# The ConvFFN of layer 0 by seven block products instead of eight, on one Trainium2 core

## The chip, the core and the metric

The kernel runs on one core of one Trainium2 chip. The metric is device time in microseconds for one execution, from the inputs in DRAM to the output in DRAM. The kernel before took 1979.17 us, the median of three runs (1978.67 to 1980.45). Engines are named as in the profile: PE (matmul), DVE, ACT, POOL (GpSimd), and SP, whose queue issues every DMA of this kernel.

## The reference

The network has two layers over 512 latent tokens and 256 context tokens of width 1024. Layer 0 mixes tokens by attention and a short convolution, layer 1 by a state-space scan; after each mixer comes a ConvFFN. The change is in the ConvFFN of layer 0, which works on all 768 tokens:

```python
def _convffn(x, w_up, conv_w, w_down):      # d = 1024, D_FF = 2816
    u = _dwconv(x @ w_up, conv_w)           # 768 x 5632, three taps along the tokens
    a, g = jnp.split(u, 2, axis=-1)         # two halves of 2816
    return (jax.nn.silu(a) * g) @ w_down    # 768 x 1024
```

Its input is normed and modulated (a scale and a shift per feature, one pair for latent and one for context tokens); its output is normed, gated and added to the stream. The modulation vectors come from products of the condition vectors with `mod_w`; those of layer 1 and the last of layer 0 are computed by the kernel while other work runs.

## The kernel before, in words

**Precision.** Every large product is made of three: each operand is held as a high part (fp32r, rounded by ACT) and the rest (low = operand − high, by DVE), and `mm3` (L133) adds high·high, high·low and low·high in PSUM. `split` (L141) is one ACT copy and one DVE subtraction; both write the arena `arena_r`, while loaded data and intermediates stand in `arena_f`. A 128 x 1024 weight block of 512 KB comes by one DMA into a ring of four slots, `self.raw`, and is split from there.

**Order.** The code is written in program order, and a scheduler sets the order on each engine. Each engine then runs its list in order: an instruction that waits holds up all behind it, and so does a DMA issue on SP.

**Side work.** `mod_tile` (L253) loads a 512 KB block of transposed `mod_w` and makes one multiply-and-sum on DVE (L259) per condition. A generator hands these out: `set_fill` names the chunks, `pump` takes the next tile, and `drain` takes all that are left. `mod_rows` (L302) does the same by matmuls with 32 columns for three chunks of layer 0, during the input projections.

**Input projections of layer 0 (93 to 230 us).** Twelve feature blocks of 128 columns, `proj(6)` to `proj(17)`, over all 768 tokens; each takes one 512 KB block `hyb_w` and 24 matmuls of 512 and 24 of 256 columns. `pump` between them takes two `mod_rows` steps for each group of three blocks.

**ConvFFN of layer 0, `ffn(0)` (456 to 1009 us).** The feature blocks come in 22 pairs (p and 22 + p). For each block `gemm_fm` takes the 8 blocks of the contraction and the 768 tokens as 512 + 256 columns: 48 matmuls in PSUM. From PSUM, ACT applies the middle tap and DVE the two others (`taps`, one instruction of 511 and one of 255 columns per tap). ACT makes the silu and DVE the product, then split. Groups of 2 to 4 pairs are multiplied at once with their rows of `ffn_down` (6 token tiles x 2 halves of 512 columns), and DVE adds the result to `macc`. All features stay in SBUF. `pump(2)` after each block takes two mod tiles. At the start, the transposed input comes in two calls of `to_hT`: four token tiles at the end of `mixer0`, two in `rest_hT` inside `ffn`. `ffn(1)` runs the same code on 512 tokens.

Of the kernel before, what the change touches and what calls it, by code (L numbers as in the profile page):

```python
# [93 lines left out]
class Kern:  # L94
# [27 lines left out]
    def dma(self, out, in_):  # L122
        return self.nc.sync.dma_start(out=out, in_=in_).ins
# [6 lines left out]
    def mm(self, out, a, b, start, stop):  # L130
        self.nc.tensor.matmul(out, a, b, start=start, stop=stop)  # L131

    def mm3(self, out, a, b, start, stop):  # L133
        self.mm(out, a[0], b[0], start, False)
        self.mm(out, a[0], b[1], False, False)
        self.mm(out, a[1], b[0], False, stop)
# [60 lines left out]
    def build(self):  # L197
        tc = self.tc
        with ExitStack() as ctx:
# [13 lines left out]
            self.yd = dram.tile([2 * D, NL], F32, name="y_dram")  # L213
            b = Bump(self.F, 0, self.NF)
# [25 lines left out]
            self.sinks()  # L240
            self.mixer0()
            if self.stop == "mix0":
                return
            self.ffn(0)
# [5 lines left out]
            self.ffn(1)  # L250


    def mod_tile(self, l, j, f, conds, cols):  # L253

        r = self.raw()
# [70 lines left out]

    def set_fill(self, chunks):
        def gen():
            for ch in chunks:
                yield from self.mod_chunk(*ch)  # L330
        self.drain()
        self.fill = gen()
# [62 lines left out]
    def mixer0(self):  # L395
# [148 lines left out]
        self.fill = self.mod_rows((4, 3, 2), cc)  # L544
# [56 lines left out]
        self.banks((0, 2, 4), (6, 7))  # L601
        rq = rows(0, 384)
# [24 lines left out]
        for j in range(4):  # L627
            ps = proj(6 + 3 * j)
            gc = tmp()
            self.act(gc, ps, AF.Copy)  # L630
            self.pump(j > 0)
            ps = proj(7 + 3 * j)
            u = tmp()
            self.tt(u, ps, gc, ALU.mult)
            y = conv32[j]
            wc = self.scw[:, 3 * j:3 * j + 3]
            self.act(y, u, scale=wc[:, 1:2])
            self.taps(y, u, wc, SEGS)
            ps = proj(8 + 3 * j)
            self.tt(y, ps, y, ALU.mult)  # L640
            self.pump(j < 3)
# [138 lines left out]
        tm2 = b.ring(512, 3)  # L780
# [32 lines left out]
        hT2 = HT(R, 8, 0, 32 * KB)  # L813
# [13 lines left out]
        for t in range(6):  # L827
            pss[t] = wo_tile(t, w1)
            if t < 4:
                fin(t)  # L830
        self.to_hT(m0[:4], hT2, 0, 1, 0, tm2)
        for t in (4, 5):
            fin(t)
        self.hT = hT2
        self.rest_hT = lambda: self.to_hT(m0[4:], hT2, NL, 1, 1, tm2, par=1)
        self.upw = [108 * KB, wb, wb + 2048]
        self.set_fill([(0, 5, (0, 1)), (1, 1, (0, 1)), (1, 0, (0, 1)), (1, 4, (0,)), (1, 3, (0,)), (1, 2, (0,)), (1, 5, (0,))])
# [18 lines left out]
    def ffn(self, l):  # L856
        io, R, F, fb = self.io, self.R, self.F, self.fb
        last = l == 1
        ntt = 4 if last else 6
        segs = SEGS[:1] if last else SEGS  # L860
        n = NL if last else NT
        hT = self.hT
        W = Ring(R, self.upw, 2048)
        if last:
            self.sinks(R[:, 120 * KB:])
        else:
            self.sinks(R[:, 104 * KB:108 * KB])
        b = Bump(R, (24 if last else 64) * KB, self.NR)
        gt = [b(2 * n) for _ in range(4)]
        wd = Ring(R, [72 * KB, 80 * KB, 16 * KB] if last else [88 * KB, 96 * KB, 116 * KB], 2048)  # L870
# [5 lines left out]
        th = ring(F, tb + 2048, 512, 2)  # L876
# [7 lines left out]
        parts = ((0, 256), (256, 512)) if last else SEGS  # L884
        ahead = (0, NPAIR, 1, NPAIR + 1) if last else (0, NPAIR, 1)
        slot = ring(self.psa, 0, 512, 5) if last else self.P
# [16 lines left out]
        self.P = Ring(self.psa, [512 * j for j in ((4, 6, 0, 2) if last else (6, 0, 2, 4))], 1024)  # L903

        def up(j):
# [12 lines left out]
            if j not in head:  # L918
                self.pump(2)
# [15 lines left out]
        def down(gi):  # L935
            grp = groups[gi]
            for t in range(ntt):
# [15 lines left out]
                if gi == len(groups) - 1:  # L953
                    finish(t)
                    if not last and t == 3:
                        self.to_hT(macc[:4], hT, 0, 0, 0, th)

        def finish(t):
            c = 0 if t < 4 else 1
# [3 lines left out]
            for h in range(2):  # L963
                s = slice(h * 512, (h + 1) * 512)
                self.tt(m[:, s], m[:, s], self.res[l, 5, c][:, s], ALU.mult, eng=self.nc.gpsimd if h == 0 else None)
                self.stt(x[:, s], m[:, s], r, x[:, s], ALU.mult, ALU.add)
                if last:
                    self.dma(self.out[t * 128:(t + 1) * 128, s], x[:, s])
            self.tap("xf%d" % l, x, slice(t * 128, (t + 1) * 128))
            if not last:  # L970
                if c == 0:
                    self.dma(self.xd[t * 128:(t + 1) * 128, :], x)
                self.norm_tok(m, x)
                if t + 4 < ntt:
                    xs.append(next_x(t + 4))
# [10 lines left out]
        for gi in range(len(groups)):  # L986
# [3 lines left out]
            if not nxt:  # L990
                for c in range(1 if last else 2):
                    self.gate_row(l, 5, c)
# [8 lines left out]
        self.rest_hT = lambda: self.to_hT(macc[4:], hT, NL, 0, 1, th, par=1)  # L1001
# [604 lines left out]
```

## Time and profile before

| | us |
|---|---|
| median of three runs | 1979.17 (1978.67 to 1980.45) |
| the profiled execution | 1985.27 |
| its span | 1983.5 |
| PE busy | 1862.7 (94%) |
| DVE busy | 1295.8 (65%) |
| ACT busy | 869.6 (44%) |
| POOL busy | 457.3 (23%) |
| moved by DMA | 226.13 MB, mean 114 GB/s |

The span runs from the first instruction to the last on the core; the rest of the execution's time lies around it. Busy time is the time in which an engine has at least one instruction running. The share of an engine is an average over stages that have different limits, so the stretches of the kernel are looked at one by one. A row of a group of instructions tells its line, engine, operation, output and inputs, shapes and count, then the total busy time and the mean time of one in ns, then the idle time in front of them and what ended it.

### The profile page before, as it was taken

What the parts mean: (1) busy time and instruction counts of PE and PEld (TensorE: products, weight loads), DVE (VectorE), ACT (ScalarE), POOL (GpSimd) and SP (SyncE); (2) the same over time, 40 slices, a digit from 0 to 9 for tenths busy, and PEclk for the clock granted to TensorE, in tenths of its full rate; (3) what the DMA queues carried; (4) which work ended last, traced back from release to release, by engine and by line L of the source; (5) the groups of instructions that cost most, each with busy time, mean ns of one, the idle gap of its engine ahead of it and who ended that gap; (6) DMA issues with size and microseconds to landing.
All of it is one profiled execution on the core that took longest, in us unless ns stands there. A gap on an engine that the chain in (4) does not pass through costs nothing.

```text
span 1983.5 us, 26291 instructions
## 1 busy us (share of the span) xinstructions
PE 1862.7 (94%) x10184; PEld 1584.8 (80%) x10184; DVE 1295.8 (65%) x1867; ACT 869.6 (44%) x1398; POOL 457.3 (23%) x514
## 2 busy tenths in 40 slices
PE   7999998899999999999989799899998899999998
PEld 3887787778888888888868688888887688888886
DVE  3332488747998667545567888878787476555564
ACT  4421367545422222322356465766664455233332
POOL 1000124111000000000040778777684110000002
PEclk9899999999999999999989989998999999999999
DMA  8155200243555535221222313232234554223322
GB/s 320 54 165 172 81 24 12 62 172 113 185 160 181 159 117 170 85 64 54 91 91 65 109 56 104 87 115 87 95 123 149 188 196 132 75 95 96 96 85 74
DMA packets 72933, 226.13 MB, mean 114 GB/s; under 512 B 9004, under 2 KB 11368, under 8 KB 72808
## 3 DMA queue, kind: packets, MB, share of 16 engines
q1 hardware_dynamic: 72808, 224.45, 34.4%
q8 instruction: 80, 1.31, 0.3%
q14 instruction: 45, 0.37, 0.1%
HBM read 210.63 MB, written 13.79 MB: 113 GB/s over the span
## 4 chain that ended last, share of the span: by engine, by line
issue 47%; PE 24%; POOL 10%; DVE 9%; DMA 5%; ACT 4%; SPq 0%; POOLq 0%; DVEq 0%; ACTq 0%
PE psum L131 23%; POOL arena_f L113 8%; DVE arena_r L113 4%; DVE arena_f L113 2%; ACT arena_f L101 2%; POOL arena_f L1292 2%; DMA arena_f<-a_dram 2%; ACT arena_r L101 1%; PE psum L139 1%; DVE arena_f L107 1%; DVE arena_f L110 1%; DMA y_dram<-arena_f 1%; DVE arena_f L697 1%; ACT junk L101 1%; POOL arena_f L107 1%
## 5 line engine op out<-in xcount | busy, mean ns | idle before, releaser
L131 PE MATMUL psum<-arena_r 128*128 128x512 f32 (+2 forms) x9324 | 1776.9, 350 | 74.4 <-ACT arena_r L101 30.4
L131 PEld LDWEIGHTS psum<-arena_r 128*128 128x128 f32 x9324 | 1504.1, 192 | 323.0 <-ACT arena_r L101 43.3
L101 ACT ACTIVATE arena_r<-arena_f 128x512 fp32r<-128x512 f32 (+5 forms) x545 | 418.5, 794 | 627.1 <-PE psum L131 279.6
L113 DVE TENSOR_TENSOR arena_r<-arena_f,arena_r 128x1024 fp32r<-128x1024 f32 (+4 forms) x497 | 482.4, 988 | 321.2 <-ACT arena_r L101 319.2
L113 POOL TENSOR_TENSOR arena_f<-arena_f 128x256 f32<-128x256 f32 (+5 forms) x330 | 313.3, 972 | 180.9 <-ACT arena_f L101 79.5
L107 POOL TENSOR_SCALAR arena_f<-arena_f 128x1 f32<-128x1 f32 (+2 forms) x88 | 37.7, 429 | 1093.2 <-ACT junk L101 987.6
L113 DVE TENSOR_TENSOR arena_f<-psum,arena_f 128x256 f32<-128x256 f32 (+6 forms) x277 | 173.9, 645 | 124.5 <-PE psum L131 109.6
L110 DVE SCALAR_TENSOR_TENSOR arena_f<-psum,arena_f 128x511 f32<-128x511 f32 (+2 forms) x356 | 217.4, 648 | 51.4 <-ACT arena_f L101 49.1
L101 ACT ACTIVATE arena_f<-psum,arena_f 128x768 f32<-128x768 f32 (+2 forms) x217 | 163.8, 764 | 95.2 <-PE psum L131 41.2
L113 DVE TENSOR_TENSOR arena_f<-arena_f 128x512 f32<-128x512 f32 (+5 forms) x180 | 144.5, 812 | 57.2 <-POOL arena_f L1292 30.1
L101 ACT ACTIVATE arena_f<-arena_f 128x512 f32<-128x512 f32 (+5 forms) x115 | 81.6, 712 | 161.3 <-DVE arena_f L110 93.0
L139 PE MATMUL psum<-arena_f 128*128 128x128 f32 x596 | 94.6, 283 | 33.8 <-DVE arena_f L107 20.9
L101 ACT ACTIVATE arena_f<-psum 128x512 f32<-128x512 f32 (+9 forms) x135 | 72.4, 547 | 97.0 <-PE psum L131 84.8
L139 PEld LDWEIGHTS psum<-arena_f 128*128 128x128 f32 x596 | 71.1, 143 | 51.1 <-DVE arena_f L107 25.8
L259 DVE SCALAR_TENSOR_TENSOR junk<-arena_f 128x1024 bf16<-128x1024 f32 x80 | 97.7, 1221 | 19.4 <-DMA arena_f<-in_mod_t_dram 18.3
L113 POOL TENSOR_TENSOR arena_r<-arena_f,arena_r 128x768 fp32r<-128x768 f32 (+2 forms) x28 | 50.0, 1803 | 247.2 <-ACT arena_r L101 232.4
L107 DVE TENSOR_SCALAR arena_f<-arena_f 128x512 f32<-128x512 f32 (+4 forms) x97 | 55.3, 611 | 28.2 <-POOL arena_f L113 27.5
L101 ACT ACT_TABLE_LOAD x48 | 61.6, 1283 | 22.9 <-DVE arena_f L110 19.5
L101 ACT ACTIVATE junk<-arena_f 128x512 bf16<-128x512 f32 (+1 forms) x76 | 40.4, 533 | 47.2 <-DVE arena_f L113 33.5
L1292 POOL TENSOR_SCALAR_AFFINE_SELECT arena_f<-arena_f 128x512 f32<-128x512 f32 x64 | 59.3, 941 | 0.0
L110 DVE SCALAR_TENSOR_TENSOR arena_f<-arena_f 128x512 f32<-128x512 f32 (+3 forms) x75 | 48.5, 683 | 10.4 <-POOL arena_f L113 5.8
L101 ACT ACTIVATE arena_r<-psum 128x512 fp32r<-128x512 f32 (+2 forms) x72 | 41.2, 591 | 30.0 <-PE psum L139 16.1
(25 smaller groups left out, 249.2 us busy)
## 6 DMA issues: line engine op xcount, KB each, us to landing
arena_f<-in_ffn_up_dram SPq DMA_DIRECT2D x88, 512.0 KB
arena_f<-in_mod_t_dram SPq DMA_DIRECT2D x56, 512.0 KB
arena_f<-in_ffn_down_dram SPq DMA_DIRECT2D x44, 512.0 KB
arena_f<-in_mod_dram SPq DMA_DIRECT2D x40, 512.0 KB
arena_f<-a_dram SPq DMA_DIRECT2D x32, 512.0 KB
arena_f<-in_ssd_w_dram SPq DMA_DIRECT2D x24, 512.0 KB
arena_f<-in_ssd_o_dram SPq DMA_DIRECT2D x24, 512.0 KB
arena_f<-in_ssd_z_dram SPq DMA_DIRECT2D x16, 512.0 KB
```

What stands on the lines that cost most here:

```text
L101: return self.nc.scalar.activation(out=out, in_=in_, func=func, **kw).ins
L107: (eng or self.nc.vector).tensor_scalar(**kw)
L110: self.nc.vector.scalar_tensor_tensor(out=out, in0=in0, scalar=s, in1=in1, op0=op0, op1=op1)
L113: return (eng or self.nc.vector).tensor_tensor(out=out, in0=a, in1=b, op=op).ins
L131: self.nc.tensor.matmul(out, a, b, start=start, stop=stop)
L139: self.nc.tensor.transpose(out, in_, self.ident)
L259: self.nc.vector.scalar_tensor_tensor(out=self.junk2, in0=r, scalar=1.0, in1=self.cb[c], op0=ALU.mult, op1=ALU.mult, accum_out=o)
L697: nc.vector.tensor_reduce(out=nm, in_=ps.rearrange("p (i n) -> p i n", i=2), axis=AX.X, op=ALU.max, negate=True)
L1292: pool.affine_select(out=rd, in_=rd, pattern=[[0, 4], [1 - 2 * d, 128]], compare_op=ALU.is_ge, fill=0.0, base=-d, channel_multiplier=2 * d ...
```

## The change

Both products of the ConvFFN of layer 0 are cut into 2 x 2 blocks, and the four block results are made by seven block products in place of eight (Strassen's scheme in Winograd's form, with the sums of blocks made beforehand). Feature pair p holds the two blocks of the weight's columns, the contraction is halved into 4 + 4 blocks, and the 768 tokens into 384 + 384. So each of the seven products of a pair is 4 contraction blocks of `mm3` with 384 columns: 12 matmuls, 84 per pair.

- **Up.** `hop` holds the input blocks and their four sums, split, for the whole stage; `rest` makes the second half and the sums (DVE, two of the four sums on POOL). For a pair, POOL makes four sums of weight blocks (128 x 512), and ACT and DVE split seven operands. The results leave PSUM by ACT copies and by three DVE operations of 384 columns into a buffer `U`, and the taps read that buffer.
- **Gated features by way of DRAM.** The product `g1` of each pair goes to `gf_dram`; for every second pair POOL makes four sums of 384 columns and they are stored too.
- **Down.** A separate run of 7 x 11 steps after all pairs: a step loads 128 x 512 of the weight (or of its sums) and 128 x 384 of features, splits both, and makes 9 matmuls of 512 columns. `macc` is combined in PSUM and by ACT and DVE after each product. The finishing of the token tiles is written into the seventh product.
- **Sums of the down weight.** `down_forms` makes them during the input projections: 11 steps of two 512 KB loads, four POOL operations of 512 columns and two 512 KB stores to `w_dram`.
- **Side work.** The 24 `mod_rows` loads are taken two steps at a time, between the first projections; two chunks of layer 1 (16 tiles, 32 sums on DVE) follow there, and the last chunk of layer 1 moves to `ffn1`.

```diff
+    def down_forms(self, slots):
+        g = self.nc.gpsimd
+        a, b = slice(0, 512), slice(512, 1024)
+        for i in range(NPAIR // 2):
+            r = [slots(1024) for _ in range(2)]
+            for k in range(2):
+                self.dma(r[k], self.io["ffn_down"][0, (2 * i + k) * 128:(2 * i + k + 1) * 128, :])
+            self.tt(r[1][:, b], r[0][:, b], r[1][:, b], ALU.subtract, eng=g)
+            self.tt(r[0][:, b], r[0][:, a], r[0][:, b], ALU.subtract, eng=g)
...
+            for k in range(2):
+                self.dma(self.wfd[k][i * 128:(i + 1) * 128, :], r[k])
+            yield
...
-        self.fill = self.mod_rows((4, 3, 2), cc)
+        def fills():
+            yield from self.mod_rows((4, 3, 2), cc)
+            yield from self.mod_chunks([(1, 1, (0, 1)), (1, 0, (0, 1))])
+        self.fill = fills()
+        forms = self.down_forms(self.gwr)
...
-            self.pump(j > 0)
+            self.pump(2)
+            next(forms, None)
             ps = proj(7 + 3 * j)
+            self.pump(2)
+            next(forms, None)
...
             ps = proj(8 + 3 * j)
             self.tt(y, ps, y, ALU.mult)
-            self.pump(j < 3)
+            self.pump(2)
+            next(forms, None)
...
+        def rest():
...
+            for f in range(4):
+                b12[f], b22[f] = feat(1, f), feat(1, f + 4)
+                op["3", f] = hl_tile(places[16 + f])
+                self.act(v3(op["3", f][0], 3), b22[f], AF.Copy)
+                self.tt(v3(op["3", f][1], 3), b22[f], v3(op["3", f][0], 3), ALU.subtract)
+                self.tt(b22[f], b12[f], b22[f], ALU.subtract)
+                self.tt(b12[f], mv[0][:, f], b12[f], ALU.subtract, eng=pool)
+                self.tt(mv[0][:, f], b22[f], mv[0][:, f], ALU.subtract)
+                op["6", f] = hl_split(mv[0][:, f], hl_tile(places[f]))
...
-        self.set_fill([(0, 5, (0, 1)), (1, 1, (0, 1)), (1, 0, (0, 1)), (1, 4, (0,)), (1, 3, (0,)), (1, 2, (0,)), (1, 5, (0,))])
+        self.set_fill([(0, 5, (0, 1)), (1, 4, (0,)), (1, 3, (0,)), (1, 2, (0,))])
...
+        def add(i, p):
...
+            self.tt(sums[i, p], x, y, ALU.add, eng=pool)
+        def operand(n):
...
+            w = WS()
+            self.split(src, w[:, a5], w[:, b5])
+            wop[p, i] = w[:, a5], w[:, b5]
+        def product(n):
...
+            for k in range(4):
+                self.mm3(ps, [x[:, k * 128:(k + 1) * 128] for x in w], op[p, k], ...)
...
+        def glu(i):
+            ya, g1 = ys[i, 0], ys[i, 1]
+            self.act(ya, ya, AF.Silu)
+            self.tt(g1, ya, g1, ALU.mult)
...
+            self.tt(x[:, h0], g0[:, h0], g0[:, h1], ALU.add, eng=pool)
+            self.tt(x[:, h1], g0[:, h1], g1[:, h1], ALU.add, eng=pool)
...
+        for n in range(6):
+            operand(n)
+        first = [product(n) for n in range(6)]
...
+        self.rest_hT()
...
+        for n in range(6, len(seq)):
+            for m in range(n, n + 4):
+                operand(m)
...
+            after(p, i, product(n))
+            if p == "2" or n < at["1", 3] and p == "7":
+                self.pump()
...
+        for n, (p, k) in enumerate(steps[:6 * nk]):
+            ahead(n + 5)
...
+            for t in range(3):
+                self.mm3(ps[t], [x[:, t * 128:(t + 1) * 128] for x in g], w, ...)
```

SP, during the input projections: `in_mod_dram` are the `mod_rows` loads, `in_hyb_w_dram` the weight of one projection, `in_ffn_down_dram` and `w_dram` the loads and stores of `down_forms`. Before:

```order
27 L123 DMA arena_f<-in_hyb_w_dram 128x1024
28 L123 DMA arena_f<-in_mod_dram 128x1024 x3
29 L123 DMA arena_f<-in_hyb_w_dram 128x1024
30 L123 DMA arena_f<-in_mod_dram 128x1024 x4
31 L123 DMA arena_f<-in_hyb_w_dram 128x1024 x2
32 L123 DMA arena_f<-in_mod_dram 128x1024 x4
```

and now:

```order
47 L123 DMA arena_f<-in_hyb_w_dram 128x1024
48 L123 DMA w_dram_72<-arena_f 128x1024
49 L123 DMA w_dram_73<-arena_f 128x1024
50 L123 DMA arena_f<-in_mod_dram 128x1024 x3
51 L123 DMA arena_f<-in_ffn_down_dram 128x1024
52 L123 DMA arena_f<-in_mod_dram 128x1024
53 L123 DMA arena_f<-in_ffn_down_dram 128x1024
54 L123 DMA arena_f<-in_mod_dram 128x1024 x4
55 L123 DMA arena_f<-in_hyb_w_dram 128x1024
```

Between two weights of projections there stood three or four loads; now there are eight loads and two stores, and the stores wait for POOL.

DVE, at the start of the ConvFFN: `junk_67` is the output of a mod sum, `128x384` (or `128x3x128`) are splits and sums of the input, `128x512` into `arena_r` splits of weights. Before, from the end of the input's split:

```order
281 L107 TENSOR_SCALAR arena_f<-psum,arena_f 128x256
282 L113 TENSOR_TENSOR arena_r<-arena_f,arena_r 128x256 x3
283 L113 TENSOR_TENSOR arena_r<-arena_f,arena_r 128x1024 x2
284 L110 SCALAR_TENSOR_TENSOR arena_f<-psum,arena_f 128x511
285 L110 SCALAR_TENSOR_TENSOR arena_f<-psum,arena_f 128x255
286 L113 TENSOR_TENSOR arena_r<-arena_f,arena_r 128x1024
```

and now, in the middle of the input's split:

```order
320 L113 TENSOR_TENSOR arena_r<-arena_f,arena_r 128x384 x2
321 L113 TENSOR_TENSOR arena_f<-arena_f 128x3x128
322 L113 TENSOR_TENSOR arena_r<-arena_f,arena_r 128x384
323 L263 SCALAR_TENSOR_TENSOR junk_67,arena_f<-arena_f 128x1024
324 L113 TENSOR_TENSOR arena_r<-arena_f,arena_r 128x384
325 L107 TENSOR_SCALAR arena_f<-psum,arena_f 128x128
326 L113 TENSOR_TENSOR arena_f<-arena_f 128x3x128
327 L113 TENSOR_TENSOR arena_r<-arena_f,arena_r 128x384
328 L113 TENSOR_TENSOR arena_r<-arena_f,arena_r 128x512
329 L263 SCALAR_TENSOR_TENSOR junk_67,arena_f<-arena_f 128x1024
```

The list of this start, from row 285 to row 342 of DVE, has 12 mod sums among 26 splits of 384 columns, 8 sums of 384 columns and 9 splits of weights.

DVE, in the middle of the up product, before:

```order
400 L110 SCALAR_TENSOR_TENSOR arena_f<-psum,arena_f 128x511
401 L110 SCALAR_TENSOR_TENSOR arena_f<-psum,arena_f 128x255
402 L259 SCALAR_TENSOR_TENSOR junk_67,arena_f<-arena_f 128x1024
403 L113 TENSOR_TENSOR arena_f<-arena_f 128x768
404 L113 TENSOR_TENSOR arena_r<-arena_f,arena_r 128x1024
```

and now:

```order
546 L113 TENSOR_TENSOR arena_f<-arena_f 128x768
547 L113 TENSOR_TENSOR arena_r<-arena_f,arena_r 128x512 x3
548 L113 TENSOR_TENSOR arena_f<-psum,arena_f 128x384
549 L113 TENSOR_TENSOR arena_r<-arena_f,arena_r 128x512
550 L110 SCALAR_TENSOR_TENSOR arena_f<-arena_f 128x511
551 L110 SCALAR_TENSOR_TENSOR arena_f<-arena_f 128x255
552 L113 TENSOR_TENSOR arena_r<-arena_f,arena_r 128x512
```

The taps read `arena_f` where they read `psum`, and a pair has seven splits of 512 columns where it had two of 1024; POOL's list, empty there before, has four operations of 512 and on average two of 384 columns per pair.

## Rows read from the trace of the kernel before

**Rows 1.** The page's view of the span in 40 slices (busy tenths).

```profile
PE   7999998899999999999989799899998899999998
DVE  3332488747998667545567888878787476555564
POOL 1000124111000000000040778777684110000002
DMA  8155200243555535221222313232234554223322
```

**Rows 2.** Windows: us, busy us of PE, PEld, DVE, ACT, POOL (x instructions), PEclk, DMA share, GB/s.

```profile
15.00:25.00 10.00, 7.71 (x44) 2.56 (x36) 2.50 (x6) 2.48 (x4) 0.00 (x0) 1.00 1.03 406
100.00:150.00 50.00, 50.00 (x298) 40.69 (x297) 18.62 (x25) 14.79 (x21) 0.00 (x0) 1.00 0.53 167
150.00:200.00 50.00, 50.00 (x308) 39.86 (x307) 13.11 (x18) 9.16 (x13) 0.00 (x0) 1.00 0.52 180
500.00:600.00 100.00, 100.00 (x536) 86.72 (x535) 94.34 (x148) 33.03 (x36) 0.00 (x0) 1.00 0.55 172
700.00:800.00 100.00, 100.00 (x518) 85.94 (x516) 65.67 (x92) 22.12 (x25) 0.00 (x0) 1.00 0.41 132
1100.00:1500.00 400.00, 357.94 (x2258) 321.08 (x2257) 336.73 (x497) 246.95 (x374) 307.37 (x317) 0.94 0.30 97
```

**Rows 3.** Timeline of PE and of DVE around the start of the ConvFFN of layer 0.

```profile
444.64 6.74 PE L131 MATMUL psum<-arena_r 128*128 128x512 f32 x29
456.45 5.76 PE L131 MATMUL psum<-arena_r 128*128 128x512 f32 x24 [0.98 <-DVE arena_r L113]
...
446.75 0.69 DVE L113 TENSOR_TENSOR arena_f<-psum,arena_f 128x512 f32<-128x512 f32 x1 [0.21 <-ACT junk L101]
452.27 0.69 DVE L113 TENSOR_TENSOR arena_f<-psum,arena_f 128x512 f32<-128x512 f32 x1 [0.57 <-ACT junk L101]
```

**Rows 4.** Timeline of PE at the end of it.

```profile
1005.83 3.45 PE L131 MATMUL psum<-arena_r 128*128 128x512 f32 x14
1011.58 0.44 PE L139 MATMUL psum<-arena_f 128*128 128x128 f32 x2 [2.30 <-DVE arena_f L107]
```

**Rows 5.** PE's cost of one matmul: timeline near 1952, groups of 72.9:91.3 and of 100:230.

```profile
1951.70 22.04 PE L131 MATMUL psum<-arena_r 128*128 128x512 f32 x96
...
L131 PE MATMUL psum<-arena_r 128*128 128x256 f32 x120 | 14.8, 284 | 0.4 <-ACT arena_f L101 0.4
...
L131 PE MATMUL psum<-arena_f 128*32 128x512 f32 x96 | 12.2, 601 | 0.0
```

**Rows 6.** Timeline of DVE, two instructions behind one another without a wait.

```profile
524.56 1.22 DVE L113 TENSOR_TENSOR arena_r<-arena_f,arena_r 128x1024 fp32r<-128x1024 f32 x1
525.70 1.22 DVE L259 SCALAR_TENSOR_TENSOR junk<-arena_f 128x1024 bf16<-128x1024 f32 x1
...
539.63 1.14 DVE L110 SCALAR_TENSOR_TENSOR arena_f<-psum,arena_f 128x511 f32<-128x511 f32 x2
540.68 1.22 DVE L259 SCALAR_TENSOR_TENSOR junk<-arena_f 128x1024 bf16<-128x1024 f32 x1
```

**Rows 7.** Groups of DVE where POOL is idle, 1620:1960 and 500:1000.

```profile
L113 DVE TENSOR_TENSOR arena_r<-arena_f,arena_r 128x512 fp32r<-128x512 f32 x22 | 15.2, 690 | 12.6 <-ACT arena_r L101 12.6
...
L259 DVE SCALAR_TENSOR_TENSOR junk<-arena_f 128x1024 bf16<-128x1024 f32 x76 | 92.8, 1222 | 19.4 <-DMA arena_f<-in_mod_t_dram 18.3
L113 DVE TENSOR_TENSOR arena_f<-arena_f 128x768 f32<-128x768 f32 x21 | 20.1, 956 | 0.2
```

**Rows 8.** Groups of DVE and of POOL where both work, 1100:1500.

```profile
L113 DVE TENSOR_TENSOR arena_r<-arena_f,arena_r 128x512 fp32r<-128x512 f32 x103 | 97.8, 958 | 9.9 <-ACT arena_r L101 9.6
L113 DVE TENSOR_TENSOR arena_f<-psum,arena_f 128x256 f32<-128x256 f32 x125 | 48.6, 414 | 2.5 <-PE psum L131 2.3
...
L113 POOL TENSOR_TENSOR arena_f<-arena_f 128x256 f32<-128x256 f32 x169 | 148.3, 901 | 54.2 <-DVE arena_r L113 16.2 <-DVE arena_f L113 15.4 <-DMA y_dram<-arena_f 14.5
L113 POOL TENSOR_TENSOR arena_f<-arena_f 128x512 f32<-128x512 f32 x62 | 82.4, 1349 | 33.3 <-DMA arena_f<-a_dram 27.5 <-DVE arena_f L113 3.1 <-ACT arena_f L101 2.6
```

**Rows 9.** Groups of ACT, 1100:1500.

```profile
L101 ACT ACTIVATE arena_r<-arena_f 128x512 fp32r<-128x512 f32 x105 | 62.9, 625 | 57.1 <-DVE arena_f L113 27.5 <-POOL arena_f L113 18.1 <-PE psum L131 6.7
```

More of the change, by code (lines that the diff above doesn't have):

```diff
@@ L240, in build @@
             self.sinks()
+            self.mraw = self.raw
             self.mixer0()
@@ L601, in mixer0 @@
         self.banks((0, 2, 4), (6, 7))
+        next(forms)
         rq = rows(0, 384)
@@ new lines, in feat @@
+        def feat(half, f):
+            pt = self.T(384)
+            for i in range(3):
+                self.tr(pt[:, i * 128:(i + 1) * 128], m0[3 * half + i][:, f * 128:(f + 1) * 128])
+            o, p3 = mv[half][:, f], v3(pt, 3)
+            for c, s in ((0, slice(0, 3)),) if half == 0 else ((0, slice(0, 1)), (1, slice(1, 3))):
+                A, B = self.colA[1, c][:, f:f + 1], self.colB[1, c][:, f:f + 1]
+                if (f + c) % 2 if half == 0 else c == 0 and f % 2:
+                    self.ts(o[:, s], p3[:, s], A, ALU.mult, B, ALU.add)
+                else:
+                    self.act(o[:, s], p3[:, s], scale=A, bias=B)
+            return o
@@ new lines, in hl_tile, with hl_split @@
+        def hl_tile(off):
+            return R[:, off:off + 384], R[:, off + 384:off + 768]
+        def hl_split(o, t, eng=None):
+            self.act(v3(t[0], 3), o, AF.Copy)
+            self.tt(v3(t[1], 3), o, v3(t[0], 3), ALU.subtract, eng=eng)
+            return t
+        op = {}
+        first = [k * KB for k in (0, 3, 6, 9, 12, 15, 18, 24)]
+        for f in range(8):
+            op["1" if f < 4 else "2", f % 4] = hl_split(feat(0, f), hl_tile(first[f]))
+        for t in (3, 4, 5):
+            fin(t)
@@ new lines, in mixer0 @@
+        places = [k * KB for k in (30, 33, 36, 39, 21, 27, 42, 45)] + [k * 1024 for k in ()] + \
+                 [k * KB for k in range(60, 96, 3)]
+        def rest():
+            b12, b22 = {}, {}
+            pool = nc.gpsimd
+            for f in range(4):
[7 more added lines that the diff above has]
+                op["6", f] = hl_split(mv[0][:, f], hl_tile(places[f]))
+            for f in range(4):
+                op["7", f] = hl_split(b22[f], hl_tile(places[8 + f]))
+            for f in range(4):
+                op["5", f] = hl_split(b12[f], hl_tile(places[4 + f]))
+            for f in range(4):
+                x = mv[0][:, f + 4]
+                self.tt(x, mv[0][:, f], x, ALU.add, eng=pool)
+                op["4", f] = hl_split(x, hl_tile(places[12 + f]))
@@ L883, in ffn @@
         head = {}
[L884 to L886 removed]
+        parts = ((0, 256), (256, 512))
+        ahead = (0, NPAIR, 1, NPAIR + 1)
+        slot = ring(self.psa, 0, 512, 5)
         seq = [j for p in range(NPAIR) for j in (p, NPAIR + p)]
@@ L902, in ffn @@
         getw(seq[len(ahead)])
-        self.P = Ring(self.psa, [512 * j for j in ((4, 6, 0, 2) if last else (6, 0, 2, 4))], 1024)
+        self.P = Ring(self.psa, [512 * j for j in (4, 6, 0, 2)], 1024)
         def up(j):
@@ L990, in ffn @@
             if not nxt:
-                for c in range(1 if last else 2):
-                    self.gate_row(l, 5, c)
+                self.drain()
+                self.gate_row(l, 5, 0)
                 xs = [next_x(t) for t in range(4)]
```

318 lines of the change are left out of this document (270 added, 48 removed).

## The prediction, made before the changed kernel ran

> **What bounds the kernel now.** I read the page's slices first: PE is at nine tenths or more nearly everywhere, DVE has room in most slices, and POOL is idle in the second to fourth slice and in the eleventh to twentieth, which is the ConvFFN of layer 0 [rows 1]. Then I cut the span into windows. In the input projections and in the ConvFFN of layer 0 PE is busy in the whole of every window, at full clock; DVE has up to 94 us of work in 100 in the first 100 us of the ConvFFN, 66 later, and POOL nothing [rows 2]. So both stages are bounded by the number and width of matmuls, and only a stage that stays so keeps what fewer matmuls give. The stage runs from the first matmul at 456.45 [rows 3] to the end of the last at 1005.83 + 3.45 = 1009.3 [rows 4]: 552.8 us.
>
> **What the matmuls give.** 96 matmuls of 512 columns took 22.04 us, 0.230 each; 120 of 256 columns 14.8 us, 0.123 each [rows 5]. Before, the stage has 44 blocks x 8 x 3 = 1056 of each width for up and 22 x 6 x 2 x 3 = 792 of 512 for down: 1848 x 0.230 + 1056 x 0.123 = 554.9, against 552.8 in the trace. After it has 22 x 84 = 1848 of 384 columns and 7 x 11 x 9 = 693 of 512. No row has 384 columns in this form; between 0.123 and 0.230, I take the middle, 0.1765. That is 326.2 + 159.4 = 485.6, a gain of 69.3 us if PE stays the bound. Every other term is what PE then waits for.
>
> **The input projections.** Here the change adds 22 loads and 22 stores of 512 KB, moves 24 `mod_rows` loads together and adds 16 mod tiles. The stage has no idle time of PE to hide a delay, and DMA is at 0.53 of its time before [rows 2]. The crowded place is the three projections from `in_hyb_w` at SP's row 38 to row 65. Between them stand, in SP's order, 22 `mod_rows` loads, 4 weights, 7 loads and 7 stores of the sums: 40 transfers. Where DMA was saturated it moved 406 GB/s [rows 2], so one of 512 KB takes 1.29 us and the 40 take 51.6. PE's work there is 3 x (24 x 0.230 + 24 x 0.123) = 25.4 us and 44 matmuls of 32 columns at 12.2/96 = 0.127 [rows 5], 5.6 us: 31.0 in all. The difference, 20.6 us, is PE idle less what was loaded ahead. Four raw slots and one of the sums ahead are 5 x 1.29 = 6.5, so I take 14. From below it is 3 (everything that POOL's first four steps have done by 100 us frees the queue early, and the loads spread), from above 28: SP's stores wait for POOL (four operations of 1.349 us [rows 8] in each of 11 steps, 59 us), and behind them in the queue stands the next projection's weight, for which PE waits; I add 1 us for each of seven such waits. The later nine projections have 32 mod sums of 1.222 us [rows 7], 39 us of DVE beside some 70 of PE: nothing.
>
> **The start of the ConvFFN.** PE's first six products need splits of the first half of the input, all the others the second half and its sums, all made by DVE in one list (its rows 285 to 342). That list comes behind the fifth and before the sixth operation of 512 columns on PSUM of the output product; these stand at 446.75 and 452.27 [rows 3], so I start it at 449.5. An instruction behind another starts 0.08 us before the other ends (524.56 + 1.22 against 525.70 [rows 6]), so a two-input operation of 512 columns costs 0.690 − 0.08 = 0.61 [rows 7], one of 384 by the same slope 0.48, a mod sum with its readout 1.23. The list: 12 mod sums 14.8; 9 weight splits 5.5; 34 splits and sums of 384 columns 16.3; the rest (reads of the transposes, norms of the last tokens) about 7.8. That is 44.4 us. Beside POOL, which makes 8 sums in it, I add 3. So DVE ends at 497, and PE has by then made 72 of its 1848 matmuls, 12.7 us. This is the largest term: 497 − 456.45 − 12.7 = 28 us of the 69.
>
> **The up product.** Left are 1776 matmuls, 313.5 us; a pair is 84 x 0.1765 = 14.8. DVE's pair: seven splits 7 x 0.61, three reads of PSUM at about 0.41, four times two taps at 1.05 (539.63 to 540.68 [rows 6]), the product 956 − 80 ns: 10.6 us. So without a disturbance PE is the bound. Two things disturb. First, the first seven pairs have the other 25 mod sums, 30.8 us. Second, POOL makes sums: 88 of 512 at 1.349 and 44 of 384 at 1.125 (the middle of 1.349 and 0.901), 168 us in about 330, half of the time. Where POOL was busy 307 of 400 us [rows 2], DVE's 512 columns took 0.958 us and not 0.690 [rows 7, 8]; an operation with one operand in PSUM, as the taps were before and are not now, still took 0.414 for 256. So at 0.51 in place of 0.77 of the time I take 0.39 x 0.51/0.77 = 0.26 on the 9.35 us of a pair that has both inputs in SBUF: 2.4 us. The first seven pairs: 7 x 13.0 + 30.8 = 121.8 against 103.6 of PE, 18 us lost; the others, 13.0 under 14.8, nothing. From below 1 (no slowing: 7 x 10.6 + 30.8 = 105), from above 107 (below).
>
> The Trainium skill has a rule for this pair, on the page "SBUF — State Buffer", section "Who interferes with whom": a DVE instruction with both inputs in SBUF and a GpSimd one that reads SBUF share a port pair under an exclusive lock, so that the one that issues second waits for the first to end. The trace agrees that only the operations without a PSUM input are slowed, but 0.958 for 0.690 is less than the sum of both would be. It is the first rival below.
>
> **Between the products and the down product.** At the change of PE from up to down the first steps' loads come from DRAM; I take 3 us (0 to 6). A down step has 9 x 0.230 = 2.07 us of PE, 0.61 + 0.48 of DVE, under 2 x 0.625 of ACT [rows 9], and 448 KB of DMA, 216 GB/s where 406 were seen: PE-bound, 159.4 us. At the end, the latent tokens are finished while two thirds of the last product run (66 matmuls, 15 us), so the transposes that PE waited 2.30 us and more for [rows 4] come earlier: 3 us gained (5 to −3). One more table load on ACT and the last mod chunk in the ConvFFN of layer 1 lie beside matmuls.
>
> **The sum.** DVE's start ends at 497; + 313.5 + 18 + 3 + 159.4 = 990.9, 18 us before 1009.3. With 14 lost ahead and 3 gained at the end the profiled execution would be 1985.27 − 18 + 14 − 3 = 1978. That execution is 6.1 above the median of the runs; the same 7 us off 1979.17 are 1972.
>
> **The rivals.**
> - *DVE and POOL take turns in the up product (slower).* With the lock in full a pair costs DVE 10.6 + 168/22 = 18.2 us; 22 x 3.4 + 30.8 = 106 lost in place of 18, 2060. For it: taps and splits now all read SBUF twice. Against it: the 0.958 at a POOL that was busy three quarters of the time. A smaller form is likelier: a pair of 10.6 + 9.35 x 0.39 = 14.2, and 0.3 of the 0.57 us that a split waits for ACT (12.6/22 [rows 7]), seven times, 16.3: 22 x 1.5 + 30.8 = 64, 46 more than in the sum, 2018. It decides as soon as DVE's pair passes 14.8 us.
> - *The waits fold into each other (faster).* POOL's sums run in DVE's pauses, mod sums slip behind splits, and the loads spread over all projections: 1 in place of 18, 3 in place of 14: 1944. For it: DVE's 10.6 us leave 4 per pair, DMA has 0.47 of the stage free [rows 2]. Against it: each engine keeps its list.
> - *SP's queue holds up the projections (slower).* 28 in place of 14, and the mod tiles of the later nine come late too, 6 more: 1992. For it: stores wait for POOL ahead of weights in the same queue. Against it: steps of POOL 5.4 us against 8.5 of a projection.
> - *The gain and the costs cancel*, 1979.
>
> **How the numbers follow.** Below, 0.2% (4 us) is what a measurement of this kernel can tell from no change. The forecast, 1972 with its own range of 1956 to 1988, has 0.42 (0.28 faster, 0.09 within, 0.05 slower); the turns 0.23, all slower; the folding 0.24, all faster; SP's queue 0.08, slower; the cancelling 0.03, within. That makes faster 0.52, same 0.12, slower 0.36. The range reaches from the folding with some more, 1938, to the smaller form of the turns, 2012; below it is left some 0.08, above 0.12.
>
> **What would show it.** In the changed kernel's profile: PE's 384-column matmuls at 0.177 us; PE idle for some 14 us within 110 to 160 us, released by DMA or ACT behind DMA, and none later in the projections; DVE without a pause for 45 us from 450 on, and PE half idle beside it; PE waiting for DVE in the next 100 us and not after; DVE's 512-column splits at 0.8 to 0.9 us beside POOL; PE full in the down product. It is wrong if PE idles through all pairs (the turns), if the first 250 us are 25 us longer (SP), or if the clock falls in the start's gaps and stays low.

## The result, and the profile after

The changed kernel took 2080.34 us (2078.72 to 2081.43, four runs) against 1978.92 for the kernel before, run beside it: a ratio of 1.0512 (95% interval 1.0494 to 1.0530), 101 us slower. The forecast of 1972 was wrong in sign, and the time lies above the range.

Three events can be found in every kernel and cut the span where the change acts: ACT's table load for the first exponential, which closes the input projections; the first transposes for the ConvFFN, behind the attention; and the first 256-column matmul of layer 1's mixer, behind the ConvFFN. ACT's and PE's timeline of the kernel before, then of the changed one:

```profile
241.88 1.28 ACT L101 ACT_TABLE_LOAD   x1
...
451.22 1.03 PE L139 MATMUL psum<-arena_f 128*128 128x128 f32 x8
...
1042.02 2.37 PE L131 MATMUL psum<-arena_r 128*64 128x256 f32 x18
```

```profile
289.27 1.28 ACT L101 ACT_TABLE_LOAD   x1
...
497.06 0.82 PE L139 MATMUL psum<-arena_f 128*128 128x128 f32 x6
502.48 1.31 PE L131 MATMUL psum<-arena_r 128*128 128x384 f32 x3
...
1140.51 0.78 PE L131 MATMUL psum<-arena_r 128*64 128x256 f32 x2
```

So 47 us are lost by the end of the projections. The attention that follows takes its old time: to the first transposes for the ConvFFN it is 497.06 − 289.27 = 208 us, before 451.22 − 241.88 = 209. The ConvFFN with the entry into the mixer then takes 643 us where it took 591: 52 lost, where the forecast had 21 gained (18 up to its last matmul, 3 behind it). The rest of the kernel differs by 4 us.

Windows of the changed kernel (columns as in [rows 2]):

```profile
100.00:150.00 50.00, 35.15 (x157) 24.60 (x156) 17.54 (x19) 9.44 (x15) 18.00 (x14) 0.76 0.73 265
150.00:200.00 50.00, 40.24 (x190) 25.33 (x189) 8.27 (x16) 6.98 (x12) 10.69 (x9) 0.83 0.85 287
500.00:550.00 50.00, 30.46 (x137) 25.33 (x137) 49.87 (x66) 26.05 (x56) 32.86 (x25) 0.71 0.33 113
600.00:650.00 50.00, 41.04 (x208) 40.39 (x209) 49.92 (x65) 19.90 (x36) 25.32 (x16) 0.87 0.48 160
850.00:900.00 50.00, 45.90 (x259) 44.45 (x259) 44.48 (x59) 25.65 (x46) 28.79 (x19) 1.00 0.36 125
950.00:1000.00 50.00, 50.00 (x219) 41.30 (x218) 29.65 (x53) 27.44 (x55) 0.19 (x1) 0.99 0.74 237
```

In the projections PE is idle for 25 of 100 us, and the granted clock is 0.76 and 0.83 in the mean where it was 1.00 [rows 2]: the pauses cost a second time. In the ConvFFN DVE is at 48.7 to 50.0 of 50 us in the four windows from 500 to 700 us, with PE between 30 and 43. Only the down product is PE-bound, as forecast.

Groups of DVE in the changed kernel's up product, 560 to 760 us, to be set beside [rows 7, 8]:

```profile
L113 DVE TENSOR_TENSOR arena_r<-arena_f,arena_r 128x512 fp32r<-128x512 f32 x74 | 63.1, 869 | 0.0
L263 DVE SCALAR_TENSOR_TENSOR junk<-arena_f 128x1024 bf16<-128x1024 f32 x27 | 39.0, 1444 | 1.3 <-DMA arena_f<-in_mod_t_dram 1.3
L110 DVE SCALAR_TENSOR_TENSOR arena_f<-arena_f 128x511 f32<-128x511 f32 x40 | 37.9, 950 | 2.6 <-ACT arena_f L101 2.6
L110 DVE SCALAR_TENSOR_TENSOR arena_f<-arena_f 128x255 f32<-128x255 f32 x40 | 33.3, 836 | 0.0
L113 DVE TENSOR_TENSOR arena_f<-psum,arena_f 128x384 f32<-128x384 f32 x33 | 17.4, 545 | 0.1
L113 DVE TENSOR_TENSOR arena_f<-arena_f 128x8 f32<-128x8 f32 x8 | 4.6, 589 | 0.0
```

An operation of 255 columns takes 836 ns, nearly as long as one of 511; one of 8 columns takes 589. Without POOL beside them, in a run shown below (e9), the same three take 482, 749 and 162. The time added has little to do with the length. Two timelines of the same place show why, DVE's first, then POOL's:

```profile
614.34 1.22 DVE L263 SCALAR_TENSOR_TENSOR junk<-arena_f 128x1024 bf16<-128x1024 f32 x1
...
618.49 0.68 DVE L113 TENSOR_TENSOR arena_r<-arena_f,arena_r 128x512 fp32r<-128x512 f32 x1
619.09 2.31 DVE L263 SCALAR_TENSOR_TENSOR junk<-arena_f 128x1024 bf16<-128x1024 f32 x1
...
621.33 1.50 DVE L113 TENSOR_TENSOR arena_r<-arena_f,arena_r 128x512 fp32r<-128x512 f32 x1
```

```profile
618.48 3.80 POOL L113 TENSOR_TENSOR arena_f<-arena_f 128x512 f32<-128x512 f32 x2 [10.41 <-DMA arena_f<-in_ffn_up_dram]
```

The mod sum that took 1.22 us alone takes 2.31 once POOL works, and the split behind it 1.50 for 0.68: 1.9 us more in the 3.8 of POOL's two operations. That is taking turns, not a small slowing. The single operations of the whole up product say the same. Where an operation of DVE with both inputs in SBUF met no operation of POOL, it took the time of its form alone within 0.015 us (0.16 us for 8 columns, 1.21 for 1024). Where it met one, the added time lay anywhere from nothing to 1.04 to 1.13 us, and this upper end is as high for 8 columns as for 1024. A sum of 512 columns on POOL that met no such operation took 1.04 to 1.30 us.

### The profile page after: what moved, and what is told of

It is laid out like the page before. It is cut to its first block, busy times and chain, and to the rows that moved or that the text cites. A ratio compares the mean times of both kernels' runs of the same rounds, so it can differ in the third digit from the quotient of the medians.

```text
span 2078.4 us, 27163 instructions
## 1 busy us (share of the span) xinstructions
PE 1855.2 (89%) x9821; PEld 1589.9 (76%) x9821; DVE 1511.7 (73%) x2147; ACT 999.3 (48%) x1747; POOL 738.6 (36%) x698
## 5 line engine op out<-in xcount | busy, mean ns | idle before, releaser
L131 PE MATMUL psum<-arena_r 128*128 128x512 f32 (+3 forms) x8961 | 1755.5, 355 | 150.4 <-DVE arena_r L113 47.0
L113 DVE TENSOR_TENSOR arena_r<-arena_f,arena_r 128x512 fp32r<-128x512 f32 (+4 forms) x738 | 644.4, 895 | 242.2 <-ACT arena_r L101 238.6
L113 POOL TENSOR_TENSOR arena_f<-arena_f 128x256 f32<-128x256 f32 (+5 forms) x514 | 598.2, 1183 | 574.4 <-DVE arena_f L113 152.7
L101 ACT ACTIVATE arena_r<-arena_f 128x512 fp32r<-128x512 f32 (+6 forms) x782 | 511.1, 683 | 538.1 <-PE psum L131 185.6
L101 ACT ACTIVATE arena_f<-arena_f 128x768 f32<-128x768 f32 (+5 forms) x160 | 123.3, 775 | 235.6 <-DVE arena_f L110 101.9
L110 DVE SCALAR_TENSOR_TENSOR arena_f<-arena_f 128x255 f32<-128x255 f32 (+4 forms) x251 | 196.1, 820 | 33.2 <-ACT arena_f L101 24.4
L101 ACT ACTIVATE arena_f<-psum 128x384 f32<-128x384 f32 (+9 forms) x229 | 114.6, 509 | 120.8 <-PE psum L131 105.4
L101 ACT ACTIVATE arena_f<-psum,arena_f 128x512 f32<-128x512 f32 (+4 forms) x185 | 129.4, 711 | 65.8 <-PE psum L131 23.8
L110 DVE SCALAR_TENSOR_TENSOR arena_f<-psum,arena_f 128x511 f32<-128x511 f32 (+2 forms) x180 | 119.6, 685 | 35.5 <-ACT arena_f L101 34.2
L139 PEld LDWEIGHTS psum<-arena_f 128*128 128x128 f32 x596 | 72.9, 146 | 71.3 <-DVE arena_f L107 26.7
L131 PE MATMUL psum<-arena_f 128*32 128x512 f32 (+5 forms) x258 | 49.2, 533 | 12.8 <-DMA arena_f<-in_mod_dram 9.5
```

Of the source, the lines that this page charges most:

```text
L101: return self.nc.scalar.activation(out=out, in_=in_, func=func, **kw).ins
L110: self.nc.vector.scalar_tensor_tensor(out=out, in0=in0, scalar=s, in1=in1, op0=op0, op1=op1)
L113: return (eng or self.nc.vector).tensor_tensor(out=out, in0=a, in1=b, op=op).ins
L131: self.nc.tensor.matmul(out, a, b, start=start, stop=stop, **kw)
L139: self.nc.tensor.transpose(out, in_, self.ident)
```

## The experiments

The table has the median and, from each profile, the end of the projections (first exponential), and two stretches: from the first transposes for the ConvFFN to the last 384-column matmul ("up"), and from there to the mixer's 256-column matmul ("down and on").

| kernel | us | projections end | up | down and on |
|---|---|---|---|---|
| before | 1979 | 242 | | |
| changed | 2080.3 | 289.3 | 436.7 | 206.8 |
| e1 rows spread | 2077.3 | 288.2 | 433.7 | 212.5 |
| e2 forms in attention | 2108.8 | 261.1 | 428.7 | 212.2 |
| e3 mods moved in the code | 2084.6 | 292.9 | 435.4 | 207.8 |
| e4 no sums | 2016.7 | 289.9 | 359.7 | 212.4 |
| e5 forms by own queue | 2087.6 | 289.8 | 430.9 | 214.4 |
| e6 no forms | 2053.6 | 258.6 | 430.1 | 211.2 |
| e7 mods pinned | 2058.4 | 287.4 | 392.5 | 230.5 |
| e8 sums unused | 2090.5 | 291.0 | 438.6 | 210.2 |
| e9 sums on DVE | 2033.0 | 288.3 | 388.3 | 212.1 |
| e10 on DVE, pinned | 2023.6 | 285.4 | 359.6 | 234.1 |
| e11 the same, e1 and e5 | 2031.4 | 290.7 | 358.5 | 236.8 |
| e12 e11, all sums on DVE | 2034.7 | 291.3 | 358.0 | 231.5 |
| e13 rows in up, four slots | 2023.0 | 259.4 | 406.5 | 205.6 |
| e14 e13 without forms | 2007.5 | 239.8 | 406.4 | 207.6 |

**e4, POOL's sums left out.**

```diff
-            sums[i, p] = SM()
-            self.tt(sums[i, p], x, y, ALU.add, eng=pool)
+            sums[i, p] = y
```

> Changed kernel without POOL's sums in the up product: the four sums of weight blocks and the four sums of gated features per two pairs are left out, their users take one of the inputs instead; every other instruction stays. Theory E (DVE and POOL share a port to SBUF: DVE's splits of 512 columns at 0.87, taps at 0.95 and 0.84, against 0.69, 0.75 and 0.48 alone): DVE gets 75 to 90 us shorter in start and up product, the time 50 to 75 us: 2005 to 2030. Theory C alone (the mod sums): DVE stays the bound at the start, gain under 25 us, 2055 to 2075.

Measured 2016.7, with 77 us off the up product. POOL's sums cost all of that, but by contention or by making splits wait for them? The next run separates the two.

**e8, POOL makes the weight sums, nobody uses them.**

```diff
-            sums[i, p] = SM()
-            self.tt(sums[i, p], x, y, ALU.add, eng=pool)
+            self.tt(SM(), x, y, ALU.add, eng=pool)
+            sums[i, p] = y
```

> Changed kernel in which POOL still makes all its sums in the up product, but the sums of weight blocks are used by nobody: their users take one of the inputs instead (as in the run without sums), so nothing of the up product waits for POOL. Theory E (the shared port: POOL's work slows DVE, whoever uses it): DVE's splits stay at 0.85 or more, time 2065 to 2085. Theory D (latency: the splits wait for POOL's sums): as without sums, 2015 to 2030, and DVE's splits near 0.69 when they don't overlap.

2090.5, and DVE's splits, 560 to 760 us, at 1.008 us:

```profile
L113 DVE TENSOR_TENSOR arena_r<-arena_f,arena_r 128x512 fp32r<-128x512 f32 x75 | 73.8, 1008 | 0.2 <-ACT arena_r L101 0.2
```

The splits no longer waited for POOL's weight sums, and nothing was won. That leaves contention, and for the weight sums the latency theory falls. The run does not free everything of POOL: ACT's middle tap reuses the buffers of POOL's sums of gated features, and between 560 and 930 us ACT still waited 21 us for POOL and 11 for the stores of these sums.

**e9, the sums on DVE.**

```diff
-            self.tt(sums[i, p], x, y, ALU.add, eng=pool)
+            self.tt(sums[i, p], x, y, ALU.add)
```

(and the same in `glu`)

> Changed kernel with all sums of the up product on DVE in place of POOL (88 of 512 columns, 44 of 384; by 0.61 and 0.48 us 75 us more on DVE). Theory E with the port as a plain lock (an instruction of DVE waits for the end of POOL's): DVE alone loses no more than it gave up, the time stays within 2060 to 2090. If the port only slows both a little (0.26 of their length, as in the prediction), DVE's 75 us come on top of the time: 2110 to 2140.

2033.0: with some 75 us more work on DVE the kernel became 47 us faster, better than either theory said. DVE's groups of this kernel, 560 to 760 us:

```profile
L113 DVE TENSOR_TENSOR arena_r<-arena_f,arena_r 128x512 fp32r<-128x512 f32 x86 | 58.2, 688 | 0.0
L110 DVE SCALAR_TENSOR_TENSOR arena_f<-arena_f 128x511 f32<-128x511 f32 x48 | 35.8, 749 | 0.0
L113 DVE TENSOR_TENSOR arena_f<-arena_f 128x512 f32<-128x512 f32 x47 | 32.3, 690 | 1.6 <-DMA arena_f<-in_ffn_up_dram 1.6
L263 DVE SCALAR_TENSOR_TENSOR junk<-arena_f 128x1024 bf16<-128x1024 f32 x26 | 31.7, 1218 | 0.0
L110 DVE SCALAR_TENSOR_TENSOR arena_f<-arena_f 128x255 f32<-128x255 f32 x48 | 23.0, 482 | 0.0
L113 DVE TENSOR_TENSOR arena_f<-psum,arena_f 128x384 f32<-128x384 f32 x37 | 20.1, 555 | 0.0
L113 DVE TENSOR_TENSOR arena_f<-arena_f 128x8 f32<-128x8 f32 x8 | 1.3, 162 | 0.0
```

Every operation with both inputs in SBUF is back at its time alone; the one with a PSUM input has not moved (555, before 545). A sum of 512 columns costs DVE 0.690 us itself; made by POOL it took POOL 1.678 in the same stretch. And it cost DVE no less: over the whole up product DVE's operations with both inputs in SBUF took 99 us longer in the changed kernel than they take alone, 0.72 for each of POOL's 136 sums of 512 and 384 columns. In e9, with the sums, DVE is busy for 381 us of the up product in place of 409, and idle for 7 in place of 26.

**e3 and e7, mod sums into the down product.** In e3 only the place of `pump` in the code was changed; the scheduler drew all 40 sums forward again (40 of them still stood before 760 us), and the time did not change beyond its spread (2079.4 and 2089.8). Its 2025 to 2040 were expected for sums that move, so it tests neither theory. In e7 they are bound to a split of the down product:

```diff
-            if p == "2" or n < at["1", 3] and p == "7":
-                self.pump()
...
-            if k % 3 == 1:
-                self.pump()
+            if p != "5" or k < 4:
+                with self.behind(self.lasttt):
+                    self.pump()
```

> Changed kernel with the 32 mod tiles (40 sums on DVE) of the ConvFFN of layer 0 bound to come behind splits of the down product, so that the scheduler can't draw them forward as it did in the run with mods in the down product's code alone. Theory C (DVE is the bound in start and up product, each sum costs its 1.45 us there and is free in the down product): 35 to 55 us less, 2025 to 2045. Theory D (PE waits for the chain through POOL and ACT): under 15 us, 2065 to 2080.

2058.4, a smaller gain than expected: up is 44 us shorter, as theory C had it, but down is 24 longer. **e10** joins e7, e9 and the input's sums on DVE.

> Sums of the up product on DVE (2033.0), with the sums of the input on DVE too and the 32 mod tiles bound to the down product. Theory E and C together (port, then DVE's load): DVE in the up product has 7 x 0.61 + 4 x 0.61 + 2 x 0.48 + 1.2 + 4.2 + 0.9 = 14.0 us a pair against PE's 14.8, so PE is nearly the bound; 30 to 45 us less, 1988 to 2003. If DVE stays the bound in spite of that: 2010 to 2025.

Its windows:

```profile
600.00:650.00 50.00, 50.00 (x290) 50.00 (x290) 47.65 (x84) 27.51 (x48) 0.00 (x0) 1.00 0.40 128
700.00:750.00 50.00, 50.00 (x291) 50.00 (x290) 46.73 (x85) 28.14 (x48) 0.00 (x0) 1.00 0.30 106
900.00:950.00 50.00, 45.01 (x194) 35.34 (x193) 43.37 (x82) 25.73 (x48) 0.26 (x1) 1.00 0.99 355
```

The up product is now PE-bound, with DVE at 47 of 50 beside it and no POOL. The down product is not: PE waits 26 us for ACT's splits there, and ACT 51 us for the features' loads; that the mod tiles beside them fill DMA (0.99) is the likely reason, not one that a run tested. 2023.6 against the 1988 to 2003 expected; the miss is the down product, 22 us longer than in e9. The time lies in the range given for DVE as the bound of the up product, which the windows do not show.

**The projections: e1, e2, e5, e6.** e1 hands the `mod_rows` loads out as the kernel before does.

```diff
-            self.pump(2)
+            self.pump(j > 0)
             next(forms, None)
             ps = proj(7 + 3 * j)
-            self.pump(2)
+            mods(4)
```

> Changed kernel, with the 24 mod_rows loads handed out over the twelve input projections as in the kernel before, and the 16 mod tiles four at a time beside them; down_forms as in the changed kernel. Theory A (bunching: the 22 mod_rows loads pulled into three projections make DMA the bound there, and the pauses lower PE's clock): the projections, 47 us longer than before, lose 25 to 40 us of that, the kernel takes 2040 to 2055. Theory B (SP's queue: the stores of down_forms wait for POOL and hold up the weights behind them): the loads stay late wherever they stand, the kernel takes 2070 to 2085.

Only 1 us at the exponential: the bunching alone is not the cause. e5 and e6 start from e1. e5 takes SP out of the steps of `down_forms`:

```diff
-                self.dma(self.wfd[k][i * 128:(i + 1) * 128, :], r[k])
+                g.dma_start(out=self.wfd[k][i * 128:(i + 1) * 128, :], in_=r[k])
```

(and the loads likewise)

> Rows-spread kernel (2077.3) with all loads and stores of down_forms issued by POOL's own queue in place of SP's: the same transfers, the same sums, but no weight of a projection stands behind a store that waits for POOL. Theory B (order in SP's queue): the first exponential comes at 255 to 265 us, as without down_forms (258.6), time 2045 to 2060. Theory F (DMA itself: 22 MB more, and loads and stores that slow one another): the exponential stays at 280 to 290, time 2070 to 2085.

289.8: taking the steps out of SP's order won nothing. It puts them on another kind of queue too (the page of e5 lists 23 MB under `software_dynamic`), and the two effects are not shown apart. e11 has the same change and was expected at 1960 to 2003; at 2031.4 it is no better than e10. e12, with the sums of `down_forms` on DVE besides, ended at 2034.7 against e11's 2031.4, with the exponential at 291.3 and 290.7, so POOL's time in a step is not it. e6 leaves `down_forms` out; its down product reads rows of the unsummed weight:

> Rows-spread kernel (the one that took 2077.3) without down_forms at all: the 22 loads, 44 sums and 22 stores are left out, and the down product reads rows of the unsummed weight in their place. Theory B (the steps of down_forms, loads, waits and stores in SP's one queue, are what holds the projections up, whatever else stands there): the first exponential comes at 242 to 250 us as in the kernel before (288.2 with them), the kernel takes 2030 to 2040. Theory A (mod_rows and mod tiles in themselves): 265 or later, 2055 to 2065.

258.6, between the two expectations and 30 us earlier than in e1, so loads, sums and stores together make 30 of the 47 and 17 are left. e2 moved ten steps into the attention:

> Changed kernel, with ten of the eleven steps of down_forms moved from the input projections into the attention, one for every second unit (512 KB loads, POOL sums and stores alike); the mod_rows loads stay bunched. Theory A (bunching of mod_rows): 24 loads in three projections still take 24 x 1.29 = 31 us beside 31 of PE, little is left of the loss from the stores' share of DMA; the projections get 20 to 30 us shorter and the attention some 3 longer, 2050 to 2062. Theory B (SP waits for POOL before each store): all of the loss goes, projections 40 to 47 us shorter, 2035 to 2045.

The projections got 28 us shorter, but the attention 57 longer (208 to 265), and the time is 47 above the highest that was expected. The attention's work buffers overlap the two slots of `down_forms` (ACT waits 26 us there for its stores), and POOL has splits of the attention to make; how much each costs is not shown. The worst place of all.

**e13 and e14.** e13 has the sums on DVE as in e10 and gives `down_forms` four slots, so that POOL has made five of the eleven steps by 93 us and all by 146 (by 245 in the changed kernel), and takes all mod tiles as matmuls of 32 columns during the up product. With only six PSUM banks left, some block products overwrite each other, so what it computes is not the ConvFFN; the number and kind of its instructions are the same.

```diff
-        forms = self.down_forms(self.gwr)
+        forms = self.down_forms(Ring(F, [self.gwr.offs[0], self.gwr.offs[1], self.cbo, self.cbo + 1024], 1024))
...
+        self.fill = self.mod_rows2([(0, 5), (1, 1), (1, 0), (1, 4), (1, 3), (1, 2)])
```

> Sums of the up product and of the input on DVE, as in the two kernels before; all modulation vectors of the ConvFFN and of the input projections' 16 tiles now by matmuls of 32 columns during the up product (12 steps of four 512 KB loads and eight matmuls, 0.127 us each: 15 us of PE in place of 72 DVE sums, 89 us), with six PSUM banks left to the products; and down_forms with four slots in place of two, so that most of its steps run before the projections. Theory G (the projections lose to down_forms because two slots make each step 13 to 18 us long, so that loads and stores fall among the weights): with four slots the exponential comes at 245 to 262 us, and with nothing but its own loads in the down product the time is 1955 to 1985. Theory F (DMA volume in any place before the attention): the exponential at 270 or later, 1990 to 2010.

> The last kernel without down_forms (loads, sums and stores left out; the down product reads rows of the unsummed weight): what the projections take with their own loads and the mod_rows alone. The exponential at 240 to 246 us as in the kernel before (241.9) if the 16 mod tiles made the 17 us that were left without down_forms; 255 or later if something else does. The difference to the last kernel is the price of down_forms with four slots.

Without forms and tiles (e14) the projections end at 239.8, and PE has no idle time in them:

```profile
100.00:150.00 50.00, 50.00 (x298) 40.97 (x298) 19.63 (x26) 15.26 (x21) 0.00 (x0) 1.00 0.55 183
150.00:200.00 50.00, 50.00 (x312) 39.23 (x311) 12.02 (x17) 9.04 (x13) 0.00 (x0) 1.00 0.48 170
```

So the 16 mod tiles make the 17 us (19 from e6 to e14), and the forms with four slots still 20 (259.4), with two 30. The 30 were measured beside the mod tiles and the 20 without them, so how much the slots won is not shown apart. e13 as a whole, 2023.0 (ratio 1.0212, 1.0192 to 1.0231), was not the step below 1985 that theory G promised: its up product is 47 us longer than e10's though PE is busy in all of it from 550 us on. The 32-column matmuls are what it is busy with. Its groups of PE, 550 to 850 us:

```profile
L131 PE MATMUL psum<-arena_r 128*128 128x384 f32 x1493 | 269.2, 337 | 0.0
L131 PE MATMUL psum<-arena_f 128*32 128x512 f32 x144 | 28.5, 605 | 0.0
L131 PE MATMUL psum<-arena_f 128*128 128x2 f32 x80 | 9.5, 240 | 0.0
```

0.198 us each and not the 0.127 of [rows 5] that my 15 us rested on, and twice as many: the trace has two matmuls for each call on f32 data (192 in this up product for 96 calls; in the kernel before 160 for the two calls of each of 40 loads). With the small products they take 38 us in this window, some 49 in the whole up product.

No version run here beats the kernel before. Added up from the best stretch of each (239.8, 359.6, 205.6, and 208 for the attention) one would reach the mixer some 29 us before 1042, but that is an estimate, and no run holds all three: the 72 mod sums and the forms always stood in one of them.

## Why the prediction was wrong

Set beside the prediction's own terms, the changed kernel lost 33 us more in the projections (47 for 14), 59 more in the up product with its start (437 for 377, six of them for matmuls of the down product that ran early) and 15 more from there to the mixer (207 for 192). The rest gave 5 back; that is the 102 us between 1978 and the profiled 2080. Two of its signs of being wrong appeared: PE idles through all pairs, and the first 250 us are over 25 longer.

- **What the matmuls give: right.** 868 matmuls of 384 columns took 150.6 us in e9 where PE was full (700 to 850 us), 0.1735 each (0.1765 taken); 528 of 512 took 120.7 in the down product, 0.229 (0.230 taken).
- **The input projections: mis-sized, 14 taken, 47 measured.** The step compared DMA at its saturated rate with PE's work in three projections, and called the later nine free. But the 16 mod tiles there cost 17 us (e6 against e14), and the steps of `down_forms` 30 (e1 against e6). "From above 28" was too low as a bound: it priced the order in SP's queue, which e5 took away without a gain, and left out the clock, granted at 0.76 and 0.83 in the windows with the pauses. Two counts were off as well: between two weights stand ten loads and not eight, and the 44 matmuls of 32 columns are 88 in the trace, 11.2 us of PE and not 5.6, which would have made the 14 a smaller 8.5. What exactly in a step holds the weights up stays open. Bunching, SP's order and POOL's sums were each taken away and did not help alone. The transfers themselves remain a candidate (DMA is busy for 0.73 and 0.85 of the time, before 0.53 and 0.52 [rows 2]); with four slots and without the mod tiles the steps cost 20 us.
- **The start: 3 us taken for POOL beside DVE.** The splits of 384 columns took 1.015 us between 500 and 560 us, 0.55 where they met no POOL; 25 of them and 11 mod sums at 1.526 for 1.22 make some 15 us, an estimate. That again is the step below.
- **The up product: the step that failed.** I took the slowing in the mixer, 0.958 for 0.690, as a factor, scaled it by POOL's busy share to 0.26 of an operation's length, 2.4 us a pair, put none on the mod sums, and let the pairs behind the seventh cost nothing because 13.0 is under PE's 14.8. What the runs show is a wait for the other engine's instruction, which falls on short operations as on long ones. For a split the factor gives the measured 0.18 us; for the taps of 255 columns it gives 0.10, and 0.35 were measured. Against e9's times a pair loses 7 x 0.18 + 4 x 0.20 + 4 x 0.35 + 0.37 = 3.8 us, and a mod sum 0.23. With that DVE is the bound for the first 200 us. Up to the end of the seventh pair PE fell 24 us behind the forecast (186 us from its first 384-column matmul, 162 forecast), and 35 more in the later pairs (245 for 210, with the six of those early matmuls); e9, without POOL's sums, took 217 for the same. So the larger part was lost where the prediction had nothing: between 800 and 900 us a pair took 16.3 us, with DVE busy for 14.7 of it and waiting for ACT in most of the rest. How much of this waiting is contention and how much is ACT's own waiting for POOL's feature sums and their stores (14 and 16 us from 760 to 930) is not shown apart. DVE's operations in front of which its waits stand, 760 to 930 us:

```profile
L110 DVE SCALAR_TENSOR_TENSOR arena_f<-arena_f 128x511 f32<-128x511 f32 x44 | 40.9, 934 | 18.4 <-ACT arena_f L101 18.2
```

- **The first rival was the right one, with too little weight.** I gave it 0.23. Its lock in full laid all of POOL's time on DVE, 7.6 us a pair, twice the 3.8 measured; its smaller form, 16.3 us a pair, is what 800 to 900 us show. I argued against it with the mean of 0.958, which did not speak against a lock: of the 103 splits in that window 85 met POOL and waited 0.34 us on average, and most of POOL's operations there are of 256 columns [rows 8], 0.63 us each where they met no such operation of DVE. The Trainium skill ("SBUF — State Buffer", "Who interferes with whom") states an exclusive lock for this pair of instructions. The trace agrees: 2.31 and 1.50 for 1.22 and 0.68, no time added without a meeting, and e9.
- **The down product and the end: PE-bound as forecast, but 15 us too short.** PE idled 4.67 and 3.77 us at its start in place of 3 in all, and 11 us in the last product, mostly between 1078 and 1105, in waits for ACT's and DVE's operations, where the prediction had a gain of 3 us.

## What to carry to other kernels

Before moving work to an idle GpSimd, count the VectorE instructions with two SBUF inputs that will meet it: if VectorE is near the bound, the same sum on VectorE itself can be the cheaper one (here 47 us). A mean slowing taken from another stage and scaled by length fails for short instructions; look at single instructions in a timeline instead, those that met the other engine beside those that did not. That an engine's mean work per round is under the bound's time does not make its delays free: PE paused in pairs where DVE was busy for nine tenths. And a stage in which PE is full does not have room for "side" transfers merely because DMA's mean share is one half (here 47 us were lost).

## What the runs showed that was not expected

Sums moved from POOL to DVE made a DVE-bound stretch shorter (436.7 to 388.3 us). Changing where side work stands in the code moved nothing until it was tied to an instruction (e3, e7). Matmuls of 32 columns cost 0.198 us in e13 in place of 0.127; their loads came through two slots there, but no run tested whether that is the reason.
